# A mixture of experts whose weights come as tiles of 8 KB rows, with the overflow branch ahead of all eight experts

## The chip, the core and the metric

The kernel runs on one core of one Trainium2 chip. TensorE (PE) multiplies matrices, VectorE (DVE) and ScalarE (ACT) work on elements, GpSimd (POOL) has little to do here, and SyncE (SP) issues the DMA transfers that bring the weights from HBM. Each engine has its own stream of instructions; they meet at semaphores. The metric is the time of one execution on the device, in microseconds (us).

## The reference

A decoder trunk of two layers over 256 tokens of 1024 channels, in float32. The first layer has attention and a dense SwiGLU, the second has attention and the experts that this change is about:

```python
def _moe(h, w_router, w1, w3, w2):
    logits = (h @ w_router).astype(jnp.float32)
    top_v, top_i = lax.top_k(logits, TOP_K)
    wts = jax.nn.softmax(top_v, axis=-1)
    gates = jnp.einsum('bske,bsk->bse',
                       jax.nn.one_hot(top_i, N_EXPERTS, dtype=jnp.float32), wts).astype(h.dtype)
    y = jnp.zeros_like(h)
    for e in range(N_EXPERTS):
        y = y + gates[..., e:e + 1] * _swiglu(h, w1[e], w3[e], w2[e])
    return y
...
        # after the mixer of each layer
        gate = jax.nn.sigmoid(_rmsnorm(x, ple_norm[i]) @ ple_w_gate[i])
        x = x + (p[i].astype(x.dtype) @ ple_w_proj[i]) * gate
    return _rmsnorm(x, final_norm)
```

w1 and w3 are 1024 x 3584 for each expert, w2 is 3584 x 1024. Eight experts hold 352 MB of weights, and all of them are read.

## The kernel before, in words

Attention and the dense layer take the first 600 us of the span and are not touched. Then `route` counts how many tokens chose each expert, ranks the experts by that count (`cnt[0:8]` says which expert has which rank) and computes the gates (`by_rank[1]`). An expert of rank r gets room for `CAPS[r]` tokens: 96 for ranks 0 to 4, 64 for ranks 5 to 7. `TURNS = (0, 5, 1, 2, 6, 3, 4, 7)` is the order of the ranks, so the rooms come as 96, 64, 96, 96, 64, 96, 96, 64. Rank 0 stands for an expert with a fixed number in the code; the numbers of the other seven are read by SP from `cnt` (`find`, seven loads) and select the DMA's source.

An `Expert` builds a selection matrix `P`, and `gather` multiplies it with the normalized tokens `xn` into `xb` (PE `scr<-P,xn`). `PT` is its transpose. The hidden width of 3584 is worked through in four chunks of 1024, 1024, 1024 and 512 columns (`moe_chunks`). For each chunk `hidden` multiplies `xb` with w1 and w3 (PE `H<-raw,xb`, `H<-mwa,xb`, `H<-mwb,xb`, by the pool in which the weight tile lies), `hidden_tail` evicts with SiLU on ACT (`sa`, `sb`), multiplies on DVE, transposes on PE (`scr<-ident,sa`) and copies to `hT`; `output` multiplies `hT` with w2 (PE `Y<-...`). Products of a chunk are issued after the hidden products of the next chunk, so that an eviction lies under matmuls, across experts as well. After an expert's last chunk `combine` splits Y into two parts (`yh`, `yl`), multiplies both with PT (PE `scr<-yh,PT`) and adds the result, times the gate, to `x` (DVE).

The class `Stream` brings the weights: 42 tiles of 1 MB for an expert, each 128 partitions by 2048 floats, w1 and w3 in turn and then w2. A tile is a piece of the weight as it lies in HBM, so its rows in HBM are 2 rows of 1024 floats (4 KB) for each partition, or 4 rows of 512 floats (2 KB) where the chunk has 512 columns. There are 17 buffers: 5 `raw`, 2 `mwa`, 10 `mwb`. SP issues tile i as soon as the instruction that last used its buffer is past; `next_raw` hands a tile to PE. Weights outside the experts (among them `ple_w_gate`, the last square) pass through `piece`, which splits each tile in a high and a low part on ACT and DVE (`whi`, `wlo`); `ahead` queues such splits as soon as the tile is loaded and the queue's simulated clock says so.

All of it is queued by `flow`, a recording layer that puts instructions on each engine's stream in the order of a simulated time.

Between the fourth and the fifth turn stands a branch. If an expert has more tokens than its room (`cnt[8] > 0`), `beyond` repeats the work for the rest with general code; with these inputs the branch is not taken. Every engine reads `cnt` (line 1441), compares, and jumps over `beyond` (line 1466). The kernel's experts are two calls of `by_turn`, four turns each, and each call ends with everything drained.

Of the kernel before, what the change touches and what calls it, by code (L numbers as in the profile page):

```python
# [15 lines left out]
OP = mybir.AluOpType  # L16
AX = mybir.AxisListType
PSUM = bass.MemoryType.PSUM

D = 1024  # L20
S = 256
NB = 2
# [3 lines left out]
NEG = -1e30  # L26
FD = 2816
FE = 3584
NE = 8

CAPS = (96, 96, 96, 96, 96, 64, 64, 64)
# [6 lines left out]
PLE_AT = 2  # L38
# [113 lines left out]
class Stream:  # L152
# [3 lines left out]
    def __init__(self, nc, act, vec, flow, rawp, look, width, nraw=NRAW):  # L156
        self.nc = nc
        self.act = act
        self.vec = vec
        self.flow = flow  # L160
        self.hls = []
        self.look = look
        self.width = width
        self.phase(0)
        self.part = None
        self.specs = []
        self.loaded = 0
        self.conv = 0
        self.used = 0
        self.raw = {}  # L170
        self.ready = {}
        self.times = {}
        self.dma = 3000.0
        self.done = {}
        self.pools = []
        self.more(rawp, nraw, "raw", -1)
# [44 lines left out]
    def load(self, upto):  # L221
        dma = self.nc.sync.dma_start
        while self.loaded < min(upto, len(self.specs)):
            src, gain = self.specs[self.loaded]
            if callable(src):
                src = src()
            t, before = self.buffer(self.loaded)
            c, n = src.shape[1], int(np.prod(src.shape[2:]))
            if len(src.shape) == 3:
                dma(t[:, :c * n].rearrange("p (c n) -> p c n", c=c), src)  # L230
            else:
                v = t[:, :c * n].rearrange("p (c t n) -> p c t n", c=c, t=src.shape[2])
                for k in range(src.shape[2]):
                    dma(v[:, :, k, :], src[:, :, k, :])
            self.raw[self.loaded] = (t, c, n, before, gain)
            self.loaded += 1
# [16 lines left out]
    def next_raw(self, held=0):  # L253

        i = self.used
        self.ahead_raw(i - held)
        self.load(i + 1)
        t, c, n, before, _ = self.raw.pop(i)
        self.landed(t, c * n, before)
        self.used += 1  # L260
        self.skip_raw()
        if self.conv < self.loaded:
            self.flow.start(self.ahead(self.loaded, i - held))
        return t[:, :c * n].rearrange("p (c n) -> p c n", c=c)

# [70 lines left out]
def trunk(ctx, tc, x, p, attn_norm, ffn_norm, a_w_qkv, a_w_o, kv_norm, kv_w, b_w_q, b_sinks,  # L336
# [4 lines left out]
    flow = Flow()  # L341
# [31 lines left out]
    def rows(w, r0, nr, c0, ncol):  # L373
        return w[r0:r0 + nr, c0:c0 + ncol].rearrange("(c p) n -> p c n", p=128)

    which = {}

    def expert_rows(w, e, *a):

        if isinstance(e, int):  # L380
            return rows(w[0, e], *a)
        return lambda: rows(w[0, bass.ds(which[e[0]], 1)].rearrange("e r n -> (e r) n"), *a)

    def add_square(s, w, gain=None):
        for k in range(2):
# [21 lines left out]
    def add_moe(s, seq, at=None, extra=None):  # L407


        prev = None  # L410
        where = 0
        for j, item in enumerate(list(seq) + [None]):
            if item is not None:
                e, f0, fn = item
                nr = s.width * 128 // fn
                for r in range(0, D, nr):
                    for w in (moe_w1, moe_w3):
                        s.add(expert_rows(w, e, r, nr, f0, fn), "raw")
            if j == at:
                s.add(extra, "raw")  # L420
                where = len(s.specs)
            if prev is not None:
                e, f0, fn = prev
                for r in range(0, fn, s.width * 128 // D):
                    s.add(expert_rows(moe_w2, e, f0 + r, s.width * 128 // D, 0, D), "raw")
            prev = item
        return where

    dense_chunks = [(0, 256)] + [(256 + 512 * i, 512) for i in range(5)]
    moe_chunks = [(0, 1024), (1024, 1024), (2048, 1024), (3072, 512)]  # L430

    def moe_seq(es):
        return [(e, f0, fn) for e in es for f0, fn in moe_chunks]

    def dense_seq():
        return [(dense_w1[0], dense_w3[0], dense_w2[0], f0, fn) for f0, fn in dense_chunks]

# [12 lines left out]
    add_square(st, b_w_o[0])  # L450
    moe0 = len(st.specs)
    ranks = [(r,) if r else 0 for r in TURNS]
    add_moe(st, moe_seq(ranks[:4]))
    moe_cut = add_moe(st, moe_seq(ranks[4:]), 3 * len(moe_chunks) + PLE_AT, rows(ple_w_proj[1], 0, 256, 0, D))
    add_square(st, ple_w_gate[1], gcol[:, 5, :])


# [844 lines left out]
    def experts(es, nxt=None, then={}, ahead=True):  # L1302

        E = {}
        nf = len(moe_chunks)

        def begin(i):
            E[i] = es[i]()
            return E[i].gather()

        def products(i, res, f, Y):
            output(E[i], Y, res, moe_chunks[f][1], f == 0, f == nf - 1)
            if f == nf - 1:
                flow.start(E[i].combine(Y, nxt if i == len(es) - 1 else None))

        prev = None
        for i in range(len(es)):
            if i not in E:
                g = begin(i)
                if not E[i].ready:  # L1320
                    flow.spawn(g)
            Y = [psY.tile([128, 512], F32, name=f"Y{k}", tag=f"Y{k}") for k in (range(3) if E[i].ng == 3 else (0,))]
            for f, (f0, fn) in enumerate(moe_chunks):
                res = []
                g = begin(i + 1) if ahead and f == nf - 2 and i + 1 < len(es) else None
                hidden(E[i], fn, res)
                if (i, f) in then:
                    then[i, f]()
                if not ahead:
                    products(i, res, f, Y)  # L1330
                    continue
                if g is not None:
                    flow.spawn(g)
                if prev is not None:
                    products(*prev)
                prev = (i, res, f, Y)
            if not ahead:
                flow.drain()
        if ahead:
            products(*prev)  # L1340
        flow.drain()

    def route():
# [15 lines left out]
            warm(WARM2)  # L1359
        first.append(Expert(CAPS[0], posm[:, :, 0:1], by_rank[1][:, :, 0:1]))  # L1360
        vec.tensor_copy(count, ps[:, 16:24])
        yield from first[0].gather()

        d8, a8, perm = d4[:, 0], a4[:, 0], d4[:, 1]
        vec.tensor_copy(total, count)
# [20 lines left out]
        vec.tensor_tensor(total, count, capx, op=OP.subtract)  # L1386
        vec.tensor_reduce(rstat[:, 0:1], total, axis=AX.X, op=OP.max)
        vec.tensor_scalar(cnt[:, 8:9], rstat[:, 0:1], 0.0, None, op0=OP.max)
        ranked.append(True)
        yield flow.now + 1.0  # L1390
        for tb in range(NB):
            vec.tensor_scalar(lg[:, tb], lg[:, tb], n_f1.r[tb], None, op0=OP.mult)
        vec.tensor_reduce(rstat[:, 1:3], lg, axis=AX.X, op=OP.max)
        vec.tensor_tensor(gates, lg, rstat[:, 1:3][:, :, None].to_broadcast([128, NB, NE]), op=OP.subtract)
        act(gates, gates, AF.Exp)
        yield flow.due(gates)
        vec.tensor_tensor(gates, gates, sel, op=OP.mult)
        vec.tensor_reduce(rstat[:, 3:5], gates, axis=AX.X, op=OP.add)
        vec.reciprocal(rstat[:, 5:7], rstat[:, 3:5])
# [11 lines left out]
        psB = pool(f"psS{k}", 2, ps, space=PSUM)  # L1411

    first = []
    ranked = []

    def by_turn(turns, then={}, **kw):

# [4 lines left out]

    def find():

        flow.until(lambda: ranked)
        for r in TURNS:
            if r:
                which[r] = nc.values_load(cnt[0:1, r:r + 1], engines=(mybir.EngineType.SP,), min_val=0, max_val=NE - 1,
                                          skip_runtime_bounds_check_because="the number of an expert")
# [1 line left out]
    st.ahead_raw(st.used)  # L1431
    moes = ExitStack()
    flow.start(route())
    flow.until(lambda: first and len(first[0].ready) == 2)
    gst.close()
    banks.close()
    expert_pools(moes, banks, 1)
    by_turn(TURNS[:4], {(0, 0): find})


    most = nc.values_load(cnt[0:1, 8:9], min_val=0, max_val=S,
                          skip_runtime_bounds_check_because="a count of at most 256 tokens")
    st.ahead_raw(st.used)
    main = st
    moes.close()
    banks.close()

    def beyond(i):

# [14 lines left out]
        selp = sel1  # L1464

    with tc.If(most > 0):
        beyond(1)
        with tc.If(most > CAP):
            beyond(2)
    ppp = pool("ppp", 1, side="right")  # L1470
    expert_pools(moes, banks, 3)


    n_p1 = Norm(div=2)
# [18 lines left out]
    def proj_p1():  # L1493
        nonlocal xtpool
        flow.until(lambda: pT1)
        w = st.next_raw()
        for tb in range(NB):
            pp = ppp.tile([128, D], F32, name="pp", tag=f"pp{tb}")
            for n in range(2):
                t = scr()  # L1500
                for c in range(2):
                    mm(t, pT1[0][:, 2 * tb + c, :], w[:, c, half(n)], start=c == 0, stop=c == 1)
                act(pp[:, half(n)], t, AF.Copy, scale=0.5)
            pps1.append(pp)
        st.ahead_raw(st.used)
        mws.close()
        st.more_split(pool("hl2", NHL), NHL)
        xtpool = pool("xT2", 1)
        st.phase(6)

    by_turn(TURNS[4:], {(3, PLE_AT - 1): load_p1, (3, PLE_AT): proj_p1}, nxt=n_p1.half)
    st.phase(7)
    moes.close()
    banks.close()
# [68 lines left out]
        "ple_norm", "ple_w_gate", "ple_w_proj", "final_norm"]  # L1583


# [16 lines left out]
```

## Time and profile before

| | us |
|---|---|
| median of 3 runs (lowest to highest) | 1558.57 (1557.28 to 1560.46) |
| the profiled execution | 1557.69 |
| its span, first to last instruction | 1555.9 |
| PE busy | 1507.0 (97%) |
| DVE, ACT, POOL busy | 541.2, 433.9, 11.3 |
| mean granted TensorE clock | 0.984 |

The profiled execution is a single run with its own time, so what is summed from its rows is set against 1557.69. [...] An engine's idle time matters only where that engine sets the end.

### The profile page before, as it was taken

Reading aid. Unit: us, or ns where it says so; the run is one execution under the profiler, and the core shown is the slowest. Engines: PE = TensorE matmul, PEld = TensorE weight load, DVE = VectorE, ACT = ScalarE, POOL = GpSimd, SP = SyncE. Lnnn points to the kernel's source line nnn. Section 1 sums busy time; section 2 is a strip of 40 time slices with the busy share of each in tenths; the row PEclk is TensorE's granted clock in tenths of the full one; section 3 lists DMA queues with packets and bytes.
Section 4 is the critical chain, followed back from the end, with each engine's and each line's share of the span. In section 5 each row is a group of like instructions: output and inputs, shape, how many; then the busy total and the mean of one; then the engine's idle time right before and its main releaser. Section 6 shows DMA issues by size and latency. Waiting matters only on the chain. (4 is left out here: it accounts for less than half of the span.)

```text
span 1555.9 us, 28406 instructions
## 1 busy us (share of the span) xinstructions
PE 1507.0 (97%) x11944; PEld 862.5 (55%) x11944; DVE 541.2 (35%) x1274; ACT 433.9 (28%) x851; POOL 11.3 (1%) x22
## 2 busy tenths in 40 slices
PE   7999999999999999999999999996999999999977
PEld 7999989888888887334333343332343343343325
DVE  6776767654545796200100100202001001201124
ACT  5555555554444775100000000100000010001123
POOL 0000000000000000000000000000000000000000
PEclk9999999999999999999999999997999999999998
DMA  9544445475554442999999999999799999999890
GB/s 280 154 142 143 122 122 170 136 253 186 175 204 162 136 131 78 410 403 408 409 402 408 408 402 409 409 402 382 299 402 408 409 402 409 406 405 408 353 338 28
DMA packets 214583, 455.66 MB, mean 293 GB/s; under 512 B 15440, under 2 KB 97232, under 8 KB 214448
## 3 DMA queue, kind: packets, MB, share of 16 engines
q1 hardware_dynamic: 214128, 453.31, 78.3%
q8 instruction: 95, 1.56, 0.4%
q0 software_dynamic: 176, 0.40, 0.1%
q14 instruction: 40, 0.33, 0.1%
q10 hardware_dynamic: 144, 0.07, 0.0%
HBM read 452.69 MB, written 1.05 MB: 292 GB/s over the span
## 5 line engine op out<-in xcount | busy, mean ns | idle before, releaser
L1137 PE MATMUL H<-mwb,xb 128*32 128x512 f32 (+1 forms) x3176 | 322.9, 540 | 0.2 <-DMA mwb<-in_moe_w 0.2
L135 DVE TENSOR_TENSOR wlo<-raw,whi 128x768 fp32r<-128x768 f32 (+1 forms) x180 | 188.5, 1079 | 117.8 <-ACT whi L135 117.5
L135 DVE TENSOR_TENSOR sa<-sa,H 128x512 f32<-128x512 f32 (+1 forms) x32 | 19.9, 621 | 574.6 <-PE H L1137 574.6
L1137 PEld LDWEIGHTS H<-mwb,xb 128*32 128x32 f32 x3176 | 104.9, 110 | 194.3 <-issue 169.7
L135 ACT ACTIVATE whi<-raw 128x768 fp32r<-128x768 f32 (+1 forms) x180 | 162.0, 945 | 111.0 <-PE scr L347 61.3
L135 ACT ACTIVATE sa<-H 128x512 f32<-128x512 f32 (+1 forms) x32 | 17.4, 544 | 611.0 <-PE H L1137 611.0
L1137 PE MATMUL H<-raw,xb 128*32 128x512 f32 (+1 forms) x1480 | 158.8, 546 | 0.0
L1137 PE MATMUL Y<-mwb,hT 128*32 128x512 f32 x1240 | 143.4, 594 | 0.0
L347 PE MATMUL acc<-whi,xT0h 128*128 128x384 f32 (+2 forms) x296 | 103.8, 351 | 0.0
L347 PE MATMUL acc<-wlo,xT0h 128*128 128x384 f32 (+2 forms) x296 | 101.4, 343 | 1.4 <-DVE wlo L135 1.4
L347 PE MATMUL acc<-whi,xT0l 128*128 128x384 f32 (+2 forms) x296 | 101.2, 342 | 0.1
L1137 PEld LDWEIGHTS H<-raw,xb 128*32 128x32 f32 x1480 | 49.4, 110 | 90.7 <-issue 79.7
L1137 PE MATMUL Y<-raw,hT 128*32 128x512 f32 x856 | 99.7, 593 | 0.0
L347 PE MATMUL acc<-whi,xT1h 128*128 128x384 f32 (+2 forms) x280 | 98.2, 351 | 0.3 <-ACT xT1h L135 0.3
L347 PE MATMUL acc<-whi,xT1l 128*128 128x384 f32 (+2 forms) x280 | 93.7, 335 | 0.2 <-DVE xT1l L135 0.2
L347 PE MATMUL acc<-wlo,xT1h 128*128 128x384 f32 (+2 forms) x280 | 93.4, 334 | 0.0
L1137 PEld LDWEIGHTS Y<-mwb,hT 128*32 128x32 f32 x1240 | 39.3, 110 | 83.5 <-issue 81.3
L1137 PE MATMUL H<-mwa,xb 128*32 128x512 f32 (+1 forms) x720 | 82.7, 531 | 0.0
L1137 PEld LDWEIGHTS Y<-raw,hT 128*32 128x32 f32 x856 | 27.5, 110 | 58.7 <-issue 57.0
L347 PEld LDWEIGHTS acc<-whi,xT0h 128*128 128x128 f32 x296 | 56.3, 190 | 4.6 <-issue 2.3
L347 PEld LDWEIGHTS acc<-wlo,xT0h 128*128 128x128 f32 x296 | 56.3, 190 | 4.1 <-DVE wlo L135 2.0
L347 PEld LDWEIGHTS acc<-whi,xT0l 128*128 128x128 f32 x296 | 56.1, 190 | 2.9 <-DVE xT0l L135 0.3
(222 smaller groups left out, 1867.4 us busy)
## 6 DMA issues: line engine op xcount, KB each, us to landing
mwb<-in_moe_w SPq DMA_DIRECT2D x190, 1024.0 KB, 18.3
raw<-in_moe_w SPq DMA_DIRECT2D x104, 1024.0 KB, 18.2
mwa<-in_moe_w SPq DMA_DIRECT2D x42, 1024.0 KB, 18.3
raw<-in_a_w_qkv SPq DMA_DIRECT2D x144, 256.0 KB, 4.0
raw<-in_dense_w SPq DMA_DIRECT2D x33, 1024.0 KB, 5.0
raw<-in_ple_w_gate SPq DMA_DIRECT2D x8, 1024.0 KB, 9.1
raw<-in_a_w_o SPq DMA_DIRECT2D x4, 1024.0 KB, 5.1
raw<-in_b_w_q SPq DMA_DIRECT2D x4, 1024.0 KB, 5.1
```

The lines of the kernel that those rows point to most:

```text
L135: f(*a, **k)
L347: nc.tensor.matmul(dst, lhsT, rhs, **kw)
L1137: nc.tensor.matmul(dst, xs, w, start=start, stop=stop)
```

## The change

Three edits. The host lays w1, w3 and w2 of the experts out again before the launch, as [expert, tile, 128, 2048]: each tile is contiguous, with one row of 8 KB for each partition. What is computed from a tile, and in which order tiles come, stays. The branch moves ahead of the experts: `route` is drained up to the ranking, every engine reads `cnt[8]` and branches, and only then all eight turns follow in a single `by_turn`; the gates (`find_gates`) and SP's seven loads (`find`) come behind the branch. And `st.hold` keeps the splits of `ple_w_gate` from being queued until the hT of the last turn is.

```diff
+MOE_CHUNKS = ((0, 1024), (1024, 1024), (2048, 1024), (3072, 512))
...
@@ class Stream: load @@
             src, gain = self.specs[self.loaded]
-            if callable(src):
-                src = src()
             t, before = self.buffer(self.loaded)
+            if isinstance(src, tuple):
+
+                src, c = src
+                src = src() if callable(src) else src
+                m = src.shape[1]
+                dma(t[:, :m], src)
+                self.raw[self.loaded] = (t, c, m // c, before, gain)
+                self.loaded += 1
+                continue
             c, n = src.shape[1], int(np.prod(src.shape[2:]))
...
@@ class Stream: next_raw @@
-        if self.conv < self.loaded:
+        if self.conv < self.loaded and not self.hold:
             self.flow.start(self.ahead(self.loaded, i - held))
...
-    def expert_rows(w, e, *a):
-
+    def expert_tile(w, e, at, n):
+
+
+        t, c = divmod(at, 2048)
         if isinstance(e, int):
-            return rows(w[0, e], *a)
-        return lambda: rows(w[0, bass.ds(which[e[0]], 1)].rearrange("e r n -> (e r) n"), *a)
+            return w[e, t][:, c:c + n]
+        return lambda: w[bass.ds(which[e[0]], 1), t].rearrange("e p n -> (e p) n")[:, c:c + n]
...
     ranks = [(r,) if r else 0 for r in TURNS]
-    add_moe(st, moe_seq(ranks[:4]))
-    moe_cut = add_moe(st, moe_seq(ranks[4:]), 3 * len(moe_chunks) + PLE_AT, rows(ple_w_proj[1], 0, 256, 0, D))
+    moe_cut = add_moe(st, moe_seq(ranks), (NE - 1) * len(MOE_CHUNKS) + PLE_AT, rows(ple_w_proj[1], 0, 256, 0, D))
     add_square(st, ple_w_gate[1], gcol[:, 5, :])
...
         def products(i, res, f, Y):
-            output(E[i], Y, res, moe_chunks[f][1], f == 0, f == nf - 1)
+            if i == len(es) - 1 and f == nf - 1:
+
+                flow.until(lambda: res)
+                st.hold = False
+            output(E[i], Y, res, MOE_CHUNKS[f][1], f == 0, f == nf - 1)
...
@@ route @@
         vec.tensor_copy(count, ps[:, 16:24])
-        yield from first[0].gather()
+        flow.start(first[0].gather())
...
         vec.tensor_scalar(cnt[:, 8:9], rstat[:, 0:1], 0.0, None, op0=OP.max)
-        ranked.append(True)
-        yield flow.now + 1.0
+
+    def find_gates():
+
+        lgr, a8, perm = gates, a4[:, 0], d4[:, 1]
...
     flow.start(route())
-    flow.until(lambda: first and len(first[0].ready) == 2)
+    flow.drain()
     gst.close()
     banks.close()
-    expert_pools(moes, banks, 1)
-    by_turn(TURNS[:4], {(0, 0): find})
 
 
     most = nc.values_load(cnt[0:1, 8:9], min_val=0, max_val=S,
                           skip_runtime_bounds_check_because="a count of at most 256 tokens")
-    st.ahead_raw(st.used)
     main = st
-    moes.close()
-    banks.close()
...
     with tc.If(most > 0):
+        find_gates()
         beyond(1)
         with tc.If(most > CAP):
             beyond(2)
     ppp = pool("ppp", 1, side="right")
-    expert_pools(moes, banks, 3)
+    expert_pools(moes, banks, 1)
+    find_gates()
+    find()
...
@@ proj_p1 @@
         st.phase(6)
-
-    by_turn(TURNS[4:], {(3, PLE_AT - 1): load_p1, (3, PLE_AT): proj_p1}, nxt=n_p1.half)
+        st.hold = True
+
+    by_turn(TURNS, {(NE - 1, PLE_AT - 1): load_p1, (NE - 1, PLE_AT): proj_p1}, nxt=n_p1.half)
...
+def _expert_tiles(w, rows):
+
+
+    out = []
+    for f0, fn in MOE_CHUNKS:
+        v = w[0][:, f0:f0 + fn] if rows else w[0][:, :, f0:f0 + fn]
+        k = 2048 // v.shape[2]
+        v = v.reshape(NE, -1, k, 128, v.shape[2]).transpose(0, 1, 3, 2, 4)
+        out.append(v.reshape(NE, -1, 128, 2048))
+    return np.ascontiguousarray(np.concatenate(out, 1))
...
+    for name in ("moe_w1", "moe_w3", "moe_w2"):
+        arrays["in_" + name] = _expert_tiles(arrays["in_" + name], name == "moe_w2")
```

On PE, the place where the experts begin. `scr<-P,xn` is the end of the first expert's gather, `scr<-ident,P` the transposes of P, H the first hidden products. Before:

```order
L347 MATMUL scr<-P,xn_5687 128x96
L347 MATMUL scr<-P,xn_5688 128x96
L1137 MATMUL H_6228<-raw,xb 32x512 x4
L1137 MATMUL H_6229<-raw,xb 32x512 x4
L1137 MATMUL H_6230<-raw,xb 32x512 x4
L352 MATMUL scr<-ident,P 96x128 x2
L1137 MATMUL H_6228<-raw,xb 32x512 x4
```

and in the changed kernel (the second run of rows is the end of the skipped blocks and what follows them):

```order
L356 MATMUL scr<-P,xn_5688 128x96
L361 MATMUL scr<-ident,P 96x128 x2
L1454 TENSOR_LOAD cnt
L1476 COMPARE_AND_BRANCH
...
L1479 UNCONDITIONAL_BRANCH x2
L1476 UNCONDITIONAL_BRANCH
L1149 MATMUL H_20316<-raw,xb 32x512 x4
L1149 MATMUL H_20317<-raw,xb 32x512 x4
L1149 MATMUL H_20318<-raw,xb 32x512 x4
```

The load of the count and the branch now stand between the gather and the first H product, and the transposes of P stand ahead of them instead of inside H.

On PE again, the handover from the fourth turn to the fifth. Y is the fourth turn's last output, `scr<-yh,PT` and `scr<-yl,PT` its combine. Before (the second run of rows is the jump's end, the gather of turn five and its first H):

```order
L1137 MATMUL Y_8351<-mwb,hT 32x512 x4
L1137 MATMUL Y_8350<-mwb,hT 32x512 x4
L347 MATMUL scr<-yh,PT 128x512
L347 MATMUL scr<-yl,PT 128x512
...
L347 MATMUL scr<-yl,PT 128x512
L1441 TENSOR_LOAD cnt
L1466 COMPARE_AND_BRANCH
...
L1466 UNCONDITIONAL_BRANCH
L347 MATMUL scr<-P,xn_5687 128x64
...
L1137 MATMUL H_23211<-mwb,xb 32x512 x4
L1137 MATMUL H_23212<-raw,xb 32x512 x4
```

and now:

```order
L1149 MATMUL Y_22380<-mwa,hT 32x512 x4
L1149 MATMUL H_23306<-mwb,xb 32x512 x4
L1149 MATMUL H_23307<-mwb,xb 32x512 x4
...
L356 MATMUL scr<-yh,PT 128x512
L356 MATMUL scr<-yl,PT 128x512
L1149 MATMUL H_23306<-mwb,xb 32x512 x4
L1149 MATMUL H_23307<-mwb,xb 32x512 x4
L356 MATMUL scr<-yh,PT 128x512
L356 MATMUL scr<-yl,PT 128x512
```

The combine of turn four now stands among the H products of turn five, whose gather has been queued earlier; no load and no branch is left there.

On ACT, the end of the experts. `sa` is the SiLU of the last chunk, `hT` its transposed copy, `whi` the splits of `ple_w_gate`, `yh` the first step of the last combine, `xT0h` a later step. Before:

```order
L135 ACTIVATE sa<-H_25734 128x256
L135 ACTIVATE whi<-raw,gcol 128x512
L135 ACTIVATE hT<-scr 128x256
L135 ACTIVATE whi<-raw,gcol 128x512 x11
L135 ACTIVATE yh<-Y_25300 64x512 x2
L135 ACTIVATE xT0h<-scr 128x512 x2
L135 ACTIVATE xT1h<-scr 128x512
```

and now:

```order
L136 ACTIVATE sa<-H_25731 128x256
L136 ACTIVATE hT<-scr 128x256
L136 ACTIVATE whi<-raw,gcol 128x512 x5
L136 ACTIVATE yh<-Y_25297 64x512 x2
L136 ACTIVATE whi<-raw,gcol 128x512 x5
L136 ACTIVATE xT0h<-scr 128x512
L136 ACTIVATE whi<-raw,gcol 128x512
L136 ACTIVATE xT0h<-scr 128x512
L136 ACTIVATE xT1h<-scr 128x512
```

`hT` stands ahead of all splits, `yh` behind five of them instead of twelve, and the other splits are spread among the later steps.

## Rows read from the trace of the kernel before

**Rows 1.** Windows: stretch and length, busy per engine (instructions), PEclk, DMA share, GB/s

```profile
640.00:1060.00 420.00, 419.19 (x4116) 148.22 (x4112) 47.46 (x89) 33.94 (x62) 0.00 (x0) 1.00 1.03 406
1069.43:1097.56 28.13, 15.79 (x59) 9.85 (x58) 9.21 (x16) 2.62 (x5) 1.14 (x2) 0.58 0.66 259
1503.07:1509.90 6.83, 3.40 (x16) 0.79 (x20) 3.56 (x6) 4.45 (x8) 0.00 (x0) 0.50 1.05 387
```

**Rows 2.** The page's costliest group: busy, mean ns, idle before, releaser

```profile
L1137 PE MATMUL H<-mwb,xb 128*32 128x512 f32 (+1 forms) x3176 | 322.9, 540 | 0.2 <-DMA mwb<-in_moe_w 0.2
```

**Rows 3.** SP's own waits: us in total, times, longest

```profile
SPq L230 <- PE H L1137: 210.8, 114, 9.2
```

**Rows 4.** Timeline, turn four to turn five: start, us, engine and operation [idle before]

```profile
1059.41 10.02 PE L1137 MATMUL Y<-mwb,hT 128*32 128x512 f32 x85
...
1086.48 0.25 DVE L135 TENSOR_SCALAR P<-iota,posr 128x64 f32<-128x64 f32 x1 [5.69 <-DVEq L1466]
...
1086.88 7.06 PE L347 MATMUL scr<-P,xn 128*128 128x64 f32 x32 [6.89 <-DVE P L135]
...
1097.56 1.06 PE L1137 MATMUL H<-mwb,xb 128*32 128x512 f32 x8
```

**Rows 5.** The branch and the join, line 1466: duration min/median/max, start

```profile
L1466 SPq EVENT_SEMAPHORE  x8: 17/17/17, 1080.2 to 1091.1; - x8
...
L1466 PEldq COMPARE_BRANCH  x1: 6062/6062/6062, 1079.4 to 1079.4; - x1
L1466 DVEq COMPARE_BRANCH  x1: 72/72/72, 1080.7 to 1080.7; - x1
```

**Rows 6.** Line 1441, the load of the count

```profile
L1441 PEldq TENSOR_LOAD <-cnt x1: 489/489/489, 1078.8 to 1078.8; - x1
```

**Rows 7.** Timeline of PE: half of a gather of 64 rows

```profile
706.01 2.00 PE L347 MATMUL scr<-P,xn 128*128 128x64 f32 x16
```

**Rows 8.** Timeline of PE: a combine pair between H products

```profile
1436.75 0.50 PE L347 MATMUL scr<-yh,PT 96*128 96x512 f32 x1
...
1437.41 1.07 PE L1137 MATMUL H<-mwb,xb 128*32 128x512 f32 x8
```

**Rows 9.** Timeline where the experts begin

```profile
616.43 0.88 SPq L230 DMA_DIRECT2D mwa<-in_moe_w  x2
...
627.22 0.16 DVE L135 COPY count<-acc 128x8 f32<-128x8 f32 x1
...
631.05 2.78 PE L1137 MATMUL H<-raw,xb 128*32 128x512 f32 x24
...
633.76 0.42 PE L352 MATMUL scr<-ident,P 128*96 128x128 f32 x2
...
634.57 0.16 DVE L135 COPY total<-count 128x8 f32<-128x8 f32 x1
...
638.95 0.15 DVE L135 TENSOR_SCALAR cnt<-rstat 128x1 int32<-128x1 f32 x1
```

**Rows 10.** Timeline of the experts' end

```profile
1493.69 0.44 PE L1258 MATMUL scr<-ident,sa 128*128 128x128 f32 x2
...
1505.45 0.72 ACT L135 ACTIVATE whi<-raw,gcol 128x512 fp32r<-128x512 f32 x1 [13.39 <-DMA raw<-in_ple_w_gate]
...
1506.50 3.58 PE L1137 MATMUL Y<-mwa,hT 128*32 128x512 f32 x16 [7.02 <-ACT hT L135]
...
1509.91 1.89 PE L1137 MATMUL Y<-raw,hT 128*32 128x512 f32 x16
...
1516.44 1.41 DVE L135 SCALAR_TENSOR_TENSOR x<-scr,gater,x 128x512 f32<-128x512 f32 x2
```

**Rows 11.** DMA queues, whole run: packets, MB, share of 16 engines

```profile
q1 hardware_dynamic: 214128, 453.31, 78.3%
```

**Rows 12.** DMA queues, 640 to 1060 us

```profile
q1 hardware_dynamic: 48212, 170.07, 102.3%
q8 instruction: 32, 0.52, 0.5%
```

More of the change, by code (lines that the diff above doesn't have):

```diff
@@ L168, in __init__ @@
         self.conv = 0
+        self.hold = False
         self.used = 0
@@ L414, in add_moe @@
                 e, f0, fn = item
-                nr = s.width * 128 // fn
-                for r in range(0, D, nr):
+                r0 = f0 * D // fn
+                for r in range(0, D, s.width * 128 // fn):
                     for w in (moe_w1, moe_w3):
-                        s.add(expert_rows(w, e, r, nr, f0, fn), "raw")
+                        s.add((expert_tile(w, e, (r0 + r) * fn // 128, s.width), s.width // fn), "raw")
             if j == at:
@@ L423, in add_moe, with moe_seq, dense_seq @@
                 e, f0, fn = prev
-                for r in range(0, fn, s.width * 128 // D):
-                    s.add(expert_rows(moe_w2, e, f0 + r, s.width * 128 // D, 0, D), "raw")
+                for r in range(f0, f0 + fn, s.width * 128 // D):
+                    s.add((expert_tile(moe_w2, e, r * D // 128, s.width), s.width // D), "raw")
             prev = item
         return where
+    def moe_seq(es):
+        return [(e, f0, fn) for e in es for f0, fn in MOE_CHUNKS]
+    def dense_seq():
+        return [(dense_w1[0], dense_w3[0], dense_w2[0], f0, fn) for f0, fn in dense_chunks]
     dense_chunks = [(0, 256)] + [(256 + 512 * i, 512) for i in range(5)]
-    moe_chunks = [(0, 1024), (1024, 1024), (2048, 1024), (3072, 512)]
-    def moe_seq(es):
-        return [(e, f0, fn) for e in es for f0, fn in moe_chunks]
     def dense_seq():
@@ L1304, in experts @@
         E = {}
-        nf = len(moe_chunks)
+        nf = len(MOE_CHUNKS)
         def begin(i):
@@ L1322, in experts @@
             Y = [psY.tile([128, 512], F32, name=f"Y{k}", tag=f"Y{k}") for k in (range(3) if E[i].ng == 3 else (0,))]
-            for f, (f0, fn) in enumerate(moe_chunks):
+            for f, (f0, fn) in enumerate(MOE_CHUNKS):
                 res = []
@@ L1388, in route @@
         vec.tensor_scalar(cnt[:, 8:9], rstat[:, 0:1], 0.0, None, op0=OP.max)
-        ranked.append(True)
-        yield flow.now + 1.0
+    def find_gates():
+        lgr, a8, perm = gates, a4[:, 0], d4[:, 1]
         for tb in range(NB):
-            vec.tensor_scalar(lg[:, tb], lg[:, tb], n_f1.r[tb], None, op0=OP.mult)
-        vec.tensor_reduce(rstat[:, 1:3], lg, axis=AX.X, op=OP.max)
-        vec.tensor_tensor(gates, lg, rstat[:, 1:3][:, :, None].to_broadcast([128, NB, NE]), op=OP.subtract)
+            vec.tensor_scalar(lgr[:, tb], lg[:, tb], n_f1.r[tb], None, op0=OP.mult)
+        vec.tensor_reduce(rstat[:, 1:3], lgr, axis=AX.X, op=OP.max)
+        vec.tensor_tensor(gates, lgr, rstat[:, 1:3][:, :, None].to_broadcast([128, NB, NE]), op=OP.subtract)
         act(gates, gates, AF.Exp)
-        yield flow.due(gates)
         vec.tensor_tensor(gates, gates, sel, op=OP.mult)
@@ L1413, in trunk @@
     first = []
-    ranked = []
     def by_turn(turns, then={}, **kw):
@@ L1423, in find @@
     def find():
-        flow.until(lambda: ranked)
         for r in TURNS:
```

## The prediction

> **What bounds the kernel now.** I read the windows first, because the shares over the whole span mix stages with different limits. Through the first four experts (640 to 1060 us) PE is busy 419.19 of 420.00 us at granted clock 1.00 while the DMA engines are at share 1.03 [rows 1]. Two resources run flat out side by side. Which of them gives way shows in the groups and in SP's waits: the H matmuls lost 0.2 us to weights in the whole run [rows 2], while SP, which issues the weights, stood 210.8 us behind H matmuls that had yet to free a buffer [rows 3]. So PE sets the end in this stage and the weights are just in time. The reader is to look next for stretches where PE is *not* busy. One is in the middle: from 1069.43 to 1097.56 PE is busy 15.79 of 28.13 us, at mean clock 0.58 [rows 1]. The other is the end, where PE stands 7.02 us before the last output products [rows 10].
>
> **The middle pause, which the change takes out.** The last Y matmul of turn four ends at 1059.41 + 10.02 = 1069.43; H of turn five runs at full speed again from 1097.56 [rows 4]: 28.13 us. Between them lie the combine, the load of the count, PE's branch (6.06 us [rows 5]), then a gather that waits 6.89 us more for P, which DVE could only begin 5.69 us after its own branch [rows 4], and a gather of 7.06 us at half clock. The change does the same matmuls between other products. Their price there, from full-clock rows: combine 4 pairs of 0.66 us (1437.41 − 1436.75 [rows 8]) = 2.6; gather of 64 rows in two halves of 2.00 = 4.0 [rows 7]; the transposes of P 0.4 (0.42 in [rows 9]); and the window's 59 matmuls [rows 1] less 8, 32 and 2 leave some 16 of H, 1.9 us (a group of 16 took 1.89 [rows 10]). Together 8.9, so 28.1 − 8.9 = 19.2 us go. If PE has to wait a little for the combine's evictions the gain is 18; if all overlaps better, 20.5. **Term: −19.2** (−18 to −20.5).
>
> **The front, where the branch now stands.** Before, H starts at 631.05, right behind the gather, and the ranking of the experts (634.57 to 639.10) lies under H and costs nothing [rows 9]. After, the order has no H matmul between the gather and the branch, and the count that the branch reads is the ranking's last result. So that cover is gone. Step by step: count is copied at 627.22 to 627.38 [rows 9]; the same ranking takes 638.95 + 0.15 − 634.57 = 4.53 us; the result is there at 631.9. PE loads it (0.49) and branches (6.06) [rows 5, 6]: 638.5, with issue gaps 638.8. H starts 638.8 − 631.05 = 7.75 us late. The two transposes of P no longer stand in H: −0.4. PE is idle for 7 us before it, and the rows show what follows such a stand: after the 7.02 us in the tail the clock was 0.50 from 1503.07 to 1509.90, thus 3.4 us into the resumed products [rows 1, 10], and at the middle pause the gather, at half clock, took 7.06 us against 4.0 at full, and H was at full speed only 10.7 us after the gather began [rows 4, 7]. Half clock costs half of its duration: 1.7 to 5 us; I take 2. **Term: +9.4** (7.4 to 13). Behind PE's branch stand all H products; behind DVE's and ACT's stand the gates (under 3 us of work), needed only at the first combine.
>
> SP, too, passes the branch, and the row of its eight event semaphores (1080.2 to 1091.1) [rows 5] shows that SP stood at the join for about 11 us. It will stand there until its 17 tiles have landed: four are there before the branch, and 13 from 616.4 [rows 9] at 2.59 us (below) give 650; then seven loads of expert numbers, and the next tile lands at about 657. The 17 tiles at hand are PE's work until 638.8 + 17 · 2.54 = 682 (2.54 is worked out below), so this hides. The stream itself stands still for about 4 us there (from 650 to SP's next issue), which costs something only if PE ever finds a tile missing.
>
> **The weights' layout.** From 640 to 1060 the weights' queue moved 170.07 MB in 48212 packets, 102.3% of 16 engines: 6875 us / 48212 = 143 ns for a mean of 3.53 KB. Over the whole run it is 78.3% of 16 · 1555.9 us / 214128 = 91 ns for 2.12 KB [rows 11, 12]. A line through both: 36.6 ns per KB and 13.6 ns for each packet. By that estimate one row of 8.19 KB costs 313 ns, two of 4.10 KB 327: 4% less DMA time. The other bound: the instruction queue's packets (0.52 MB / 32 = 16 KB) took 0.5% of 6720 us / 32 = 1.05 us, 64 ns per KB [rows 12], so a larger packet isn't cheaper by itself. The line is nearer in queue and kind; I take its −4%, with no gain as the near bound and 64 ns per KB as the far one. A tile of 1.05 MB takes 420 / (170.07 / 1.0486) = 2.59 us, then 2.49.
>
> Does it show? PE needs the 336 tiles in 1511.8 − 631.05 − 19.2 − 7 = 854 us, 2.54 each, the DMA 2.59 each, but it starts at 616.4 with four tiles there: (338 − 4) · 2.59 + 616.4, and 4 for SP's stand, end at 1485, and PE will want the last tile at 1509.9 − 7 − 19.2 + 9.4, about 1493. So even without any gain the stream ends 8 us ahead; with 4% it ends about 33 us earlier and SP just waits longer. In the middle it is tighter: the pause used to refill all 17 buffers, and after it comes a turn of 64 rows that eats tiles faster than they come (the 16 Y matmuls of one tile: 1.89 us [rows 10]). Without the pause and without any gain I estimate 0 to 5 us of stalls there; with 4%, none. **Term: 0** (0 to +5).
>
> [...]
>
> **The tail.** Before, ACT took the first split of the gate weights ahead of the last hT, waited 13.39 us for its DMA, and PE stood for hT; the last products ran at 1506.50 and 1509.91 and ended at 1511.80; x came at 1516.44 [rows 10]. After, hT goes first: its transposes were done at 1494.1 [rows 10], so only the weights hold Y, which ends about 7 us earlier. But x doesn't gain all of it: yh now stands behind five splits, and the fifth needs the second gate tile. It lands 1.05 MB / 387 GB/s = 2.71 us after the first (1505.4 [rows 1, 10]), at 1508.1. With steps of 0.7 (the first split took 0.72 [rows 10]) yh follows at 1508.8, yl from 1509.5 to 1510.7; then DVE has four more wlo, 2.8 us: x at 1513.5, 2.9 us earlier. Splits that now stand between the later steps and a clock that may halve at other places give back a part. **Term: −2.5** (−6 to 0).
>
> **Sum**, against the profiled execution (1557.69 us, 1.8 of them outside its span; it lies 0.9 under the median 1558.57): 1557.7 − 19.2 + 9.4 + 0 − 2.5 = 1545.4. I say **1545 us**.
>
> **Rivals.**
> *A, the weights set the pace:* DMA share 1.03 speaks for it, and then 4% of 870 us would come off too: 1510 to 1515. Against: 0.2 us lost to weights [rows 2] and SP's long waits for PE [rows 3]. 5%.
> *B, H waits at the join, the other sign:* if PE's first H needs all 17 tiles, as SP does, it starts at 651 instead of 638.8: front +22, 1557 to 1560. From a front of 22 us on nothing is won. For: SP's stand of 11 us at the join before. Against: PE's branch was over at 1079.4 + 6.06 = 1085.5 and its gather ran from 1086.88 [rows 4, 5], while SP stood until 1091.1. 6%.
> *C, starved middle:* rows of 8 KB cost no less, and the refill is gone: 0 to 8 us of stalls, 1545 to 1555, 9%; if they cost 4% more instead of less, 2.69 us a tile, the stream would end at 616.4 + 334 · 2.69 + 4 = 1519, 26 us after PE wants it: about 1570, 3%; at the instruction packets' 64 ns per KB a tile would take 8 · 524 ns = 4.2 us, and the time would be past 2000: 1%.
> *D, a cheap branch at the front:* should its target be at hand there, front +1.5 to 3: 1537 to 1539, 5%. For it: DVE's branch row itself was 72 ns. Against: DVE's next work was 5.69 us late all the same [rows 4].
> [...]
>
> **How the numbers follow.** The forecast has 71%, with its own range 1540 to 1550: front 7.4 to 13, middle −18 to −20.5, tail 0 to −6. A has 5, B 6, C 13, D 5. The range is to hold 8 in 10: with D's and C's near parts 1536 to 1555. 0.2% (3 us) is about what a measurement can tell from no change. Faster: the forecast, A, D and C's small stalls, 0.87; same: half of B, 0.05; slower: C's far end, half of B, some unseen cost, 0.08.
>
> **What the changed profile would show.** Front: PE idle about 7 us before the first H at 639, with a branch row near 6 us. Middle: no stretch of idle PE between turns four and five, clock 1.00. Layout: packets of the weights halved, tiles nearer 2.49 us, DMA share below 1 where SP waits for PE. Tail: no wait of Y for hT; yh behind the second gate tile. Wrong I am if H starts near 651 (B), if H or Y wait for DMA by several us (C), or if PE's time per tile falls (A).

## The result, and the profile after

The changed kernel takes 1544.16 us (median of 6 runs, 1543.54 to 1546.88) against 1558.49: ratio 0.9911, 95% interval 0.9901 to 0.9922, 14 us faster. 1545 was forecast. The span of the profiled execution is 1542.2 us, against 1555.9.

The front comes first, because there the change costs time. This is the timeline of the changed kernel from the gather to the fifth tile of H (start, us, engine and operation, idle before it):

```profile
626.14 3.71 PE L356 MATMUL scr<-P,xn 128*128 128x96 f32 x32
...
630.54 0.15 DVE L136 TENSOR_SCALAR cnt<-rstat 128x1 int32<-128x1 f32 x1
...
637.36 0.36 DVE L136 TENSOR_SCALAR gates<-lg,ss 128x8 f32<-128x8 f32 x2 [6.34 <-DVEq L1476]
...
637.90 11.90 PE L1149 MATMUL H<-raw,xb 128*32 128x512 f32 x96 [7.83 <-DVE gates L136]
...
649.61 5.34 PE L1149 MATMUL H<-mwa,xb 128*32 128x512 f32 x48
```

The same two places before the change, which [rows 9] does not have:

```profile
627.41 3.71 PE L347 MATMUL scr<-P,xn 128*128 128x96 f32 x32
...
641.87 5.33 PE L1137 MATMUL H<-mwa,xb 128*32 128x512 f32 x48
```

From the gather's start to the first product with a `mwa` tile it was 14.46 us and is 23.47: **+9.0**. The ranking's result stands at 630.69, the first H at 637.90. Line 1476 is the branch of the changed kernel (the same view as [rows 5]):

```profile
L1476 SPq EVENT_SEMAPHORE  x8: 17/17/17, 638.7 to 654.9; - x8
...
L1476 PEldq COMPARE_BRANCH  x1: 6232/6232/6232, 631.3 to 631.3; - x1
L1476 DVEq COMPARE_BRANCH  x1: 72/72/72, 631.4 to 631.4; - x1
...
L1476 DVEq EVENT_SEMAPHORE  x1: 21/21/21, 637.2 to 637.2; - x1
```

PE's branch row takes 6.23 us, until 637.5, and H follows 0.4 us later; the timeline names DVE's gates as the releaser, but in the run with one expert in the body DVE goes on 0.74 us behind its last work, PE's branch takes 6.07 us, and H comes behind that branch. DVE's next instruction comes at 637.2, 5.8 us after its branch. SP stands at the join until 654.9 and H does not wait for it: rival B is out. Windows of the changed kernel (the same view as [rows 1]; the last three columns are PEclk, the granted clock as a share of full speed, DMA share and GB/s):

```profile
640.00:1060.00 420.00, 419.29 (x4082) 149.76 (x4078) 46.21 (x85) 33.52 (x60) 0.00 (x0) 1.00 0.99 408
631.60:637.90 6.30, 0.00 (x1) 0.04 (x2) 0.50 (x3) 0.95 (x1) 0.00 (x0) 0.69 1.01 411
637.90:649.61 11.71, 11.71 (x96) 3.53 (x100) 1.79 (x10) 0.55 (x2) 1.14 (x2) 0.88 1.02 413
1066.30:1094.43 28.13, 28.13 (x262) 8.66 (x264) 0.98 (x2) 1.95 (x4) 0.00 (x0) 1.00 1.01 407
```

PE idles for 7.8 us up to 637.9; the mean granted clock from 631.6 on is 0.69, and in the first 11.7 us of H it is 0.88. The last row is the handover from turn four to turn five: 28.13 of 28.13 us busy at clock 1.00, where 15.79 of 28.13 stood. Work behind the front and ahead of the tail is 19.5 us shorter: the last `sa` is transposed at 1481.90 instead of 1493.69 [rows 10], 11.8 earlier, while the fifth tile came 7.7 later. **−19.5.** Of this 19.1 lie between the fourth and the fifth turn; 0.4 come at the end of the second turn, where PE had waited for weights before.

The end of the experts (the same view as [rows 10]):

```profile
1481.90 0.44 PE L1270 MATMUL scr<-ident,sa 128*128 128x128 f32 x2
...
1489.91 1.92 PE L1149 MATMUL Y<-raw,hT 128*32 128x512 f32 x16 [0.47 <-DMA raw<-in_moe_w]
...
1492.68 3.34 ACT L136 ACTIVATE whi<-raw,gcol 128x512 fp32r<-128x512 f32 x5 [9.86 <-DMA raw<-in_ple_w_gate]
...
1495.93 0.57 ACT L136 ACTIVATE yh<-Y 64x512 fp32r<-64x512 f32 x1
...
1501.61 1.41 DVE L136 SCALAR_TENSOR_TENSOR x<-scr,gater,x 128x512 f32<-128x512 f32 x2
```

Y no longer waits for hT, only 0.47 us for its tile; `yh` stands behind five splits, and x comes 19.71 us after the transposes of `sa` where it came after 22.75. To the end of the span it is 60.3 us instead of 62.2: **−1.9.** The weights' queue from 640 to 1060 us (the same view as [rows 12]):

```profile
q1 hardware_dynamic: 23393, 170.29, 98.3%
```

It took half the packets for as many MB. The stretch holds times in which no tile was due, so the speed is read from 700 to 940 us, where the stream ran without a break in both kernels, before and after:

```profile
q1 hardware_dynamic: 27364, 97.22, 102.3%
```

```profile
q1 hardware_dynamic: 13818, 100.61, 100.8%
```

A tile of 1.05 MB took 2.59 us there and takes 2.50, 3.4% less.

### The profile page after: what moved, and what is told of

The parts are those of the page before. It is cut to its first block, busy times and chain, and to the rows that moved or that the text cites. A ratio compares the mean times of both kernels' runs of the same rounds, so it can differ in the third digit from the quotient of the medians.

```text
span 1542.2 us, 28405 instructions
## 1 busy us (share of the span) xinstructions
PE 1500.6 (97%) x11944; PEld 859.4 (56%) x11944; DVE 541.3 (35%) x1274; ACT 435.2 (28%) x852; POOL 11.3 (1%) x22
## 3 DMA queue, kind: packets, MB, share of 16 engines
HBM read 452.69 MB, written 1.05 MB: 294 GB/s over the span
## 4 chain that ended last, share of the span: by engine, by line
PE 56%; DVE 1%; DMA 1%; ACT 1%; issue 0%; POOLq 0%; DVEq 0%; ACTq 0%
PE H L1149 33%; PE Y L1149 16%; PE scr L356 4%; PE scr L1270 1%; PE acc L356 1%; DMA raw<-in_ple_w_gate 1%; DVE wlo L136 0%; PE scr L361 0%; ACT xb L136 0%; DVE x L136 0%; DVE gate L136 0%; DVE h L136 0%; ACT whi L136 0%; ACT gate L136 0%; DVE xT0l L136 0%
## 5 line engine op out<-in xcount | busy, mean ns | idle before, releaser
L1149 PE MATMUL H<-mwb,xb 128*32 128x512 f32 (+1 forms) x3208 | 328.0, 539 | 0.0
L136 DVE TENSOR_TENSOR wlo<-raw,whi 128x768 fp32r<-128x768 f32 (+1 forms) x180 | 188.6, 1080 | 117.7 <-ACT whi L136 117.0
L1149 PE MATMUL Y<-mwb,hT 128*32 128x512 f32 x1192 | 138.2, 594 | 0.0
L1149 PE MATMUL H<-mwa,xb 128*32 128x512 f32 (+1 forms) x688 | 79.1, 528 | 0.0
```

Source lines behind the costliest of these rows:

```text
L136: f(*a, **k)
L1149: nc.tensor.matmul(dst, xs, w, start=start, stop=stop)
```

## The experiments

**The old rows in the new order.** Only the layout is undone.

```diff
-        s.add((expert_tile(w, e, (r0 + r) * fn // 128, s.width), s.width // fn), "raw")
+        s.add(expert_rows(w, e, r, nr, f0, fn), "raw")
```

> The changed kernel with the experts' weights left as they lie in HBM (rows of 4 KB and 2 KB); the branch ahead of the experts and the held splits stay. Theory (PE sets the pace, the layout is hidden): 1544 to 1549 us, no group of H or Y waits more than 5 us for weights, the share of the DMA engines back at 1.02 to 1.03 from 640 to 1060 us, 2.6 us a tile. Rival A (the weights set the pace, the layout is part of the gain): 25 to 35 us slower than the changed kernel, so 1570 to 1580, slower than before. Rival C (the pause refilled the buffers, and without it the old rows starve PE at the turns of 64 rows): 1549 to 1556, with the wait in the fifth or sixth turn.

Measured 1550.84 us, ratio 0.9945 (0.9931 to 0.9958): 7 us of the gain are gone, and the time lies above the theory's 1544 to 1549, in rival C's range. Windows, and PE's waits for weights in its timeline:

```profile
820.00:880.00 60.00, 58.72 (x586) 20.88 (x582) 6.61 (x10) 3.73 (x7) 0.00 (x0) 1.00 1.03 408
1139.00:1180.00 41.00, 38.16 (x396) 13.88 (x399) 0.84 (x2) 1.26 (x3) 0.00 (x0) 0.96 1.03 403
1180.00:1480.00 300.00, 299.56 (x2824) 105.33 (x2820) 38.22 (x65) 27.27 (x49) 0.00 (x0) 1.00 1.02 400
```

```profile
837.13 4.50 PE L1149 MATMUL H<-mwb,xb 128*32 128x512 f32 x40 [1.02 <-DMA mwb<-in_moe_w]
...
1160.15 1.92 PE L1149 MATMUL Y<-raw,hT 128*32 128x512 f32 x16 [0.62 <-DMA raw<-in_moe_w]
1162.80 1.06 PE L1149 MATMUL H<-mwa,xb 128*32 128x512 f32 x8 [0.73 <-DMA mwa<-in_moe_w]
1165.36 6.20 PE L1149 MATMUL H<-mwa,xb 128*32 128x512 f32 x40 [1.49 <-DMA mwa<-in_moe_w]
```

PE is idle for 2.8 us in the second stretch, and the clock falls to 0.96. This is the end of the fifth turn, of 64 rows, and the start of the sixth. So the layout isn't the pace (rival A would be 1570), but rival C's place is real: without the pause that refilled the buffers, the old rows starve PE there. From the fifth turn's last transposes of `sa` to the sixth turn's first it is 33.2 us, where the changed kernel has 28.0, so this place costs 5.2 us; the kernel before, with the same rows and the pause, took 28.0 there too. Another 1.7 are lost in the first stretch, behind the second turn, which has 64 rows too; the kernel before lost 0.4 there. No pause was taken out ahead of it. SP's stand at the join lies ahead of it (DMA share 0.34 from 650 to 660 us, 1.03 before), but that this is the reason is not shown. Together these are 6.9 us. The tail is 2.4 us longer as well, where Y waits 1.9 us for tiles instead of 0.5, and the gather began 1.3 us earlier in this profile.

**The layout alone**, in the kernel before.

> The kernel before with the new layout of the experts' weights and nothing else. Theory (PE sets the pace): as before, 1557 to 1559 us, with fewer packets, a DMA share below 1 and SP waiting longer for PE. Rival A (the weights set the pace): 1525 to 1540.

Measured 1553.67 us, 0.9967 (0.9955 to 0.9979): 5 us faster, which no theory had. Its trace says where half of it is. The branch stands in the middle again; its rows and two windows, the second from PE's branch to its end:

```profile
L1476 SPq EVENT_SEMAPHORE  x8: 17/17/17, 1075.4 to 1077.0; - x8
...
L1476 PEldq COMPARE_BRANCH  x1: 3389/3389/3389, 1079.7 to 1079.7; - x1
```

```profile
1069.78:1095.33 25.55, 15.50 (x58) 9.64 (x59) 9.21 (x16) 2.62 (x5) 1.14 (x2) 0.60 0.26 106
1079.70:1083.10 3.40, 0.63 (x2) 0.00 (x0) 1.31 (x2) 0.00 (x0) 0.00 (x0) 0.50 0.02 7
```

What the DMA queues moved in the second window, and the same window (PE's branch) in the kernel before:

```profile
q8 instruction: 1, 0.02, 1.6%
q14 instruction: 1, 0.01, 0.8%
```

```profile
1079.40:1085.50 6.10, 0.59 (x2) 0.00 (x0) 1.28 (x2) 0.00 (x0) 0.00 (x0) 0.50 0.86 334
```

PE's branch takes 3.39 us there, not 6.06, and the pause 25.55 us, not 28.13. The DMA engines are at share 0.02 during the branch, where they were at 0.86 before: the faster stream had run ahead (share 0.43 from 1072 to 1080 us), and SP was through the join at 1077.0, before PE came at 1079.7. The only packets in the window are two of the instruction queues, which the view counts on the same 16 engines as the weights' q1. In the kernel before, the same window (PE's branch) has five of them beside 519 packets of q1, which take 82.9% of those engines. I read them as the code at the branch's target. That gave a new theory, that the fetch of code waits for the weights; the run with nine tiles, below, tries it. Of the other 2 us, 0.4 lie at the end of the second turn, where PE no longer waits; the rest is not placed, and by the interval (a gain of 3.3 to 7.0 us) there may be none.

**No hold.** One line, `st.hold = True`, is taken out.

> The changed kernel without the hold: the splits of the gate weights may be queued ahead of the last hT again, as before the change. Theory (the tail's part of the gain is what the end of the trace shows, about 2 us of the 14): 1545 to 1548 us, with Y waiting about 7 us for hT behind a split that waits for its weights. Rival (the tail is worth nothing, since x waits for the second gate tile either way): 1544, no difference.

Measured 1544.90 us, 0.9911 (0.9896 to 0.9926): no difference that can be measured. The timeline shows the old order and what it costs:

```profile
1496.17 0.72 ACT L136 ACTIVATE whi<-raw,gcol 128x512 fp32r<-128x512 f32 x1 [11.88 <-DMA raw<-in_ple_w_gate]
1496.80 0.36 ACT L136 ACTIVATE hT<-scr 128x256 f32<-128x256 f32 x1
...
1497.21 3.64 PE L1149 MATMUL Y<-mwa,hT 128*32 128x512 f32 x16 [5.57 <-ACT hT L136]
...
1507.16 1.60 DVE L136 SCALAR_TENSOR_TENSOR x<-scr,gater,x 128x512 f32<-128x512 f32 x2
```

Y waits 5.57 us for hT again; the time doesn't tell the theory's 1545 to 1548 from the rival's 1544. x loses only 1.5 us by the wait: counted from the Y group behind the transposes of `sa` (1482.27 in the changed kernel, 1486.29 here) it comes after 20.87 us instead of 19.34, and the end of the span 1.1 later. Six profiles with the hold and the same tail differ by 1.3 us in that stretch (table below), so these 1.1 are no more than a sign. `yh` stands behind splits in both orders, so hT's gain is mostly lost again at the next step.

**A short body.** The branch's body keeps the gates and loses the overflow passes.

```diff
     with tc.If(most > 0):
         find_gates()
-        beyond(1)
-        with tc.If(most > CAP):
-            beyond(2)
```

> The changed kernel with the overflow passes left out of the branch's body (only the gates stay in it), so that the jump is over a few instructions on every engine; with these inputs the body isn't run, so the output is the same. Theory (the 6 us are the fetch of instructions at a target far away): the branch rows of PE, DVE and ACT fall well under 1 us, the first H comes 4.5 to 6 us earlier, 1537 to 1540 us. Rival (a branch costs 6 us by itself, near or far): no change, 1544.

Measured 1539.58 us (1535.33 to 1542.60), 0.9872 (0.9853 to 0.9891). PE's branch row and the timeline:

```profile
L1476 PEldq COMPARE_BRANCH  x1: 228/228/228, 633.4 to 633.4; - x1
```

```profile
632.60 0.15 DVE L136 TENSOR_SCALAR cnt<-rstat 128x1 int32<-128x1 f32 x1
...
633.77 10.51 PE L1149 MATMUL H<-raw,xb 128*32 128x512 f32 x96 [1.65 <-DVEq L1476]
...
644.07 1.50 PE L1149 MATMUL H<-mwa,xb 128*32 128x512 f32 x12
```

PE's branch takes 0.23 us, H comes 1.0 us behind the ranking's result instead of 7.2, and its first four tiles take 10.30 us instead of 11.71, at clock 1.00. From the gather to the fifth tile it is 15.87 us instead of 23.47. The time shows less of it (4.6 us): in this profile, which is the median run, the gather began 2.1 us later and the tail is 0.9 longer. So it is the long body that makes the 6 us here; the branch over the short one takes 0.23.

**One expert in the body.** The body keeps `beyond(1)` for a single expert.

> The changed kernel with the branch's body cut to one expert of one overflow pass (the rest of the overflow is left out; with these inputs the body isn't run). The jump is then over some 680 matmuls with their weight loads on PE, but only over a few dozen instructions on DVE and ACT. Theory (the distance decides for each engine by itself): DVE's and ACT's next instructions come within 1 us, PE's branch row stays at 5 to 7 us, and the first H and the time are as in the changed kernel, 1543 to 1546. Rival (PE reaches that far ahead): PE's branch row is short too, and the time is that of the run with the short body, 1537 to 1540.

Measured 1545.61 us, 0.9913 (0.9897 to 0.9930), as the theory had it.

```profile
L1476 PEldq COMPARE_BRANCH  x1: 6072/6072/6072, 631.4 to 631.4; - x1
```

```profile
637.76 12.00 PE L1149 MATMUL H<-raw,xb 128*32 128x512 f32 x96 [7.65 <-PEq L1476]
```

By the timeline DVE stood idle only 0.74 us at its branch and ACT 1.14; PE's branch took 6.07 us (the jump is over 606 matmuls by the program, not the 680 expected), and H waited for it, after 7.65 us without a matmul. In this run each engine paid for its own distance, and the slowest, PE with 6.07 us, set H.

**Nine tiles ahead of the branch**, eight right behind it.

```diff
+    st.limit = moe0 + 9
...
-            if turns[-n] >= low:
+            if turns[-n] >= low or self.loaded >= self.limit:
...
     find_gates()
+    st.limit = 1 << 30
+    st.ahead_raw(st.used)
```

> The changed kernel with only nine weight tiles issued ahead of the branch instead of 17; the other eight are issued right behind it, so that the DMA engines are nearly idle while PE, ACT and DVE fetch the code at the branch's target. Theory (the fetch takes 6.2 us because it shares the DMA engines with the weights, and 3.4 us where they are idle): PE's branch row 3 to 4 us, the first H about 2.5 us earlier, 1540 to 1543 us, unless the later stream starves a turn of 64 rows (its least lead was 7 us in the changed kernel). Rival (the fetch depends on the distance alone): branch row 6 us, 1544 or a little more.

Measured 1542.88 us (1541.26 to 1544.47), 0.9892 (0.9876 to 0.9909). The branch, and the window from its start to its end:

```profile
L1478 SPq EVENT_SEMAPHORE  x8: 17/17/17, 636.9 to 637.5; - x8
...
L1478 PEldq COMPARE_BRANCH  x1: 3549/3549/3549, 633.5 to 633.5; - x1
```

```profile
633.50:637.10 3.60, 0.00 (x0) 0.00 (x0) 0.00 (x0) 0.00 (x0) 0.00 (x0) 0.55 0.04 11
```

PE's branch takes 3.55 us at DMA share 0.04, where the changed kernel has 6.23 at 1.01; the edit changes only when SP issues tiles. H came 4.5 us behind the ranking instead of 7.2, and the front is 2.5 us shorter (21.00 from the gather to the fifth tile). In the time itself it is 1.3 us, too little to tell; the gather began 2.2 us later in this profile. That the branch is shorter where the weights stand still is shown by the row, a gain in the time isn't.

**Splits behind yh.** The hold ends when `yh` and `yl` of the last combine are queued.

```diff
-                flow.until(lambda: res)
-                st.hold = False
...
                 flow.start(E[i].combine(Y, nxt if i == len(es) - 1 else None))
+                if i == len(es) - 1 and st.hold:
+                    st.hold = False
+                    flow.start(st.ahead(st.loaded, st.used))
```

> The changed kernel with the splits of the gate weights held until yh and yl of the last combine are queued. Theory (in the changed kernel yh stands behind five splits, of which the fifth needs the second gate tile): yh about 3.5 us earlier against the last Y, x about 4 us earlier, and 1 to 4 us off the whole, 1540 to 1543 us. Rival (the splits themselves, some 0.65 us each on ACT and on DVE, set when the gate products can go, in whatever order): no difference beyond 1 us.

Measured 1539.98 us (1538.30 to 1541.54), 0.9878 (0.9861 to 0.9894): every run is faster than every run of the changed kernel (1542.11 is its fastest of ten, with the repeat below).

```profile
1480.39 0.44 PE L1270 MATMUL scr<-ident,sa 128*128 128x128 f32 x2
...
1488.06 1.92 PE L1149 MATMUL Y<-raw,hT 128*32 128x512 f32 x16 [0.22 <-DMA raw<-in_moe_w]
...
1490.05 0.59 ACT L136 ACTIVATE yh<-Y 64x512 fp32r<-64x512 f32 x1 [8.74 <-PE Y L1149]
...
1491.39 0.59 ACT L136 ACTIVATE yh<-Y 64x512 fp32r<-64x512 f32 x1 [0.75 <-DVE yl L136]
...
1492.00 3.17 ACT L136 ACTIVATE whi<-raw,gcol 128x512 fp32r<-128x512 f32 x5
...
1495.53 1.41 DVE L136 SCALAR_TENSOR_TENSOR x<-scr,gater,x 128x512 f32<-128x512 f32 x2
```

`yh` follows the last Y at once; x comes 15.14 us after the transposes of `sa`, where it was 19.71.

**Splits behind x**, the hold ends one step later, in `combine`.

> The same with the splits held until x is queued. Theory of the order: x still earlier, as early as yh, yl and the products with PT allow; but the splits start later and end later. If the splits bound the tail, this one is slower than the version that holds them until yh is queued, by 1 to 4 us; if x bounds it, it is as fast or faster.

Measured 1541.02 us (1539.75 to 1542.22), 0.9884 (0.9867 to 0.9900). By the time this is not to be told from the version above. By the trace its tail is no slower: x comes 13.14 us after the transposes of `sa` (15.14 above), and the end of the span 55.5 after them (56.1 above). So x gains 2.0 us, of which 0.6 are left at the end; the rest goes behind x, where the splits now stand, but the tail is not 1 to 4 us longer. What makes this profile slower lies ahead: its front took 25.0 us, against 23.6.

**The yardstick, no branch, and both edits at once.**

> The changed kernel once more, unedited, as the yardstick for the next two runs on the same chip: 1543 to 1546 us.

1544.25 us, 0.9901 (0.9885 to 0.9918).

> The changed kernel without the load of the count, the branch and the overflow passes (they are left out; with these inputs they don't run). Theory (the branch, its wait for the ranking and the clock that falls meanwhile are all that the front costs): the first H right behind the transposes of P, some 7 us earlier, full clock in the first H products, 1535 to 1538 us. Rival (the stream of weights, or the turns behind, give the 7 us back): above 1540.

1534.72 us, 0.9850 (0.9834 to 0.9866): 9.5 us under the yardstick, just below the range that was expected. From the gather to the fifth tile:

```profile
624.94 3.71 PE L356 MATMUL scr<-P,xn 128*128 128x96 f32 x32
...
628.80 10.51 PE L1149 MATMUL H<-raw,xb 128*32 128x512 f32 x96
...
639.12 5.33 PE L1149 MATMUL H<-mwa,xb 128*32 128x512 f32 x48
```

It is 14.18 us, as before the change (14.46). So the branch at the front costs 9.3 us by the traces and 9.5 by the times. The experts behind it take as long as in the changed kernel (832.1 and 832.3 us), so nothing there gives any back.

> The changed kernel with nine tiles ahead of the branch and the splits held until yh and yl are queued, both at once. If the two gains lie at different places and add: 2 to 3 us at the front, 3 to 4 us at the end, 1537 to 1540 us. If the later start of the stream is given back at a turn of 64 rows or at the end: 1540 to 1543.

1540.09 us, 0.9883 (0.9866 to 0.9899). This is the time of the hold alone; the 2 to 3 us of the nine tiles did not show on top. In the trace the front is 1.7 us shorter than with the hold alone, the experts take the same 832.3 us, so no turn of 64 rows gives it back, and the tail is 0.7 longer. The fastest full versions are the three with the splits behind `yh` or x; the times don't tell them apart.

**Where each profile's time lies.** Three marks cut a span in four: the start of the gather, the first product with a `mwa` tile, and the transposes of the last `sa`. All in us:

| profile | gather begins | front | experts | tail | span |
|---|---|---|---|---|---|
| before | 627.41 | 14.46 | 851.82 | 62.21 | 1555.9 |
| changed | 626.14 | 23.47 | 832.29 | 60.30 | 1542.2 |
| changed, once more | 627.75 | 23.89 | 832.26 | 60.90 | 1544.8 |
| old rows | 624.88 | 23.71 | 839.42 | 62.69 | 1550.7 |
| layout alone | 628.20 | 14.45 | 848.82 | 61.83 | 1553.3 |
| no hold | 627.90 | 25.69 | 832.33 | 61.38 | 1547.3 |
| short body | 628.20 | 15.87 | 832.33 | 61.20 | 1537.6 |
| one expert in the body | 626.18 | 23.40 | 832.22 | 59.90 | 1541.7 |
| no branch | 624.94 | 14.18 | 832.12 | 61.06 | 1532.3 |
| nine tiles | 628.31 | 21.00 | 832.36 | 59.93 | 1541.6 |
| splits behind yh | 624.48 | 23.60 | 832.31 | 56.11 | 1536.5 |
| splits behind x | 625.20 | 24.97 | 832.30 | 55.53 | 1538.0 |
| nine tiles and yh | 625.06 | 21.86 | 832.34 | 56.84 | 1536.1 |

With the new order and the new rows the experts take 832.1 to 832.4 us in all ten profiles, whatever stands ahead of them.

## Why the prediction was right

- *Middle.* Forecast −19.2, by the traces −19.1 at the handover, which is now seamless (28.13 of 28.13 us busy). The mechanism is the forecast one.
- *Front.* Forecast +9.4, by the traces +9.0: H comes 7.2 us behind the ranking, and the clock costs 1.4 us in the first four tiles (11.71 against 10.30), where 2 were taken. In the six other profiles with this front, that with one expert among them, it is 23.4 to 25.7 us, so +9 to +11. Taking the branch away gave 9.5. Rival D (a cheap branch) came only with the short body: 0.23 us there, 6.2 here. The runs speak for a wait for code at the branch's target: 0.23 us for a jump over almost nothing on PE, 6.07 over 606 matmuls, and packets of the instruction queues while PE stands, two of them the only packets in the 3.4 us of the layout alone.
- *Layout.* Forecast 0, with 0 to 5 us of stalls if it brought nothing. The run with the old rows showed 5.2 us of stalls at the end of the fifth turn, where the forecast had them, and 1.7 at the end of the second, where it had none. So the layout pays back what the missing pause would take. A tile takes 3.4% less time (2.59 us, now 2.50); the forecast had 4%. At the end of the second turn, where the old rows had cost 0.4 us before, this shows. What I had not seen is that the layout gains 5 us in the kernel before as well, 2.6 of them in the pause, where the branch found idle DMA engines (share 0.02, 0.86 before) and took 3.39 us instead of 6.06. The step by which PE sets the pace and the layout hides behind it missed that PE's branch, too, is longer while the weights move.
- *Tail.* Forecast −2.5, −1.9 in the trace, x 3.0 earlier (2.9 forecast). In the other five profiles with this tail it is −1.0 to −2.3. How much of it is the hold and how much the faster stream is not shown: without the hold the tail is 1.1 longer and the time no different, and with the hold and the old rows it is 62.7, no shorter than before. That `yh` would stand behind the second gate tile was right, and moving it ahead of the splits was worth 4 us more.
- *Sum.* 9.0 − 19.5 − 1.9 is −12.4, where −12.3 was forecast. Another 1.3 us came ahead of the gather, where the edit touches nothing (last section). That the sum fits to 0.1 us is luck: the front alone differs by 2 us from profile to profile.

## What to carry to other kernels

A branch whose body isn't run can still cost: look at what the engine does *next*. Here PE's jump over a long body took 6.0 to 7.0 us under the weights (DMA share 1.01 in the changed kernel), 3.4 to 3.5 where the DMA engines were nearly idle (0.02 and 0.04), and 0.2 over a short body. So try a short skipped body, or a branch at a time when DMA is quiet. And before a pause is taken out, ask what it refilled; before a hold is set, look which instruction stands behind it next.

## What the runs showed that I had not expected

The branch took PE 5.97 to 6.99 us in the eight profiles in which the weights ran and the body was long (606 matmuls or more). It took 3.39 and 3.55 us in the two in which they stood still (layout alone, nine tiles), and 3.49 in the one with both edits, where nine tiles were issued ahead of it as well (DMA share 0.82 from 629.6 to 650 us, where the hold alone has 1.01 from 629 to 650). And the clock ahead of the gather differs between executions of the same instructions: from 618 to 626 us it was 0.57 before, 0.79 in the changed kernel and 1.00 in the run with old rows, and the gather began at 627.41, 626.14 and 624.88. The changed kernel itself, run once more, began it at 627.75, with 0.81 in that stretch. Over the thirteen profiles this is a spread of 3.8 us, more than the hold or the nine tiles are worth.
